# Norm boundaries of a two-layer encoder: half of the transposing products and zero-opened accumulators in the gap, the root from sums reduced early, weight conversions held behind, upper parts first

## The chip, the cores and the metric

One core of one Trainium2 chip. The metric is the device time of one execution in microseconds (us); lower is better. The core has TensorE (PE: matrix products; its weight loads are listed as PEld), VectorE (DVE), ScalarE (ACT), GpSimd (POOL) and SyncE (SP), whose queue issues most DMAs. Products accumulate in PSUM, which this kernel uses as eight buffers of 128 x 512 fp32 numbers; everything else on the core lives in SBUF.

## The reference

256 tokens of width 2048 pass through two layers. Layer 0 mixes tokens with a convolution module, layer 1 with gated linear attention (GLA); each layer then has a feed-forward with a short convolution. Every sub-layer f is wrapped in two norms and an adaptive modulation:

```python
h = _rms_norm(x, norm_g[i, 0]) * (1.0 + scale_m) + shift_m
y = mixer(h)                                    # conv module, or GLA
x = x + gate_m * _rms_norm(y, norm_g[i, 1])
h = _rms_norm(x, norm_g[i, 2]) * (1.0 + scale_f) + shift_f
y = _conv_ffn(h, ffn_w_in[i], ffn_conv_w[i], ffn_conv_b[i], ffn_w_out[i])
x = x + gate_f * _rms_norm(y, norm_g[i, 3])
```

`_rms_norm(x, g)` divides each token by the root of the mean of its squares plus 1e-6 and multiplies by g. Everything is fp32; the matrix products have to keep nearly that precision.

## The kernel before

**Products.** A weight block of 128 x 2048 is loaded whole (1 MB) by SP and split into an upper part `hi` (ACT casts it to the matmul format fp32r) and a lower part `lo` (DVE: weight minus upper part), in halves of 1024 columns (`Stream._process`, L120 and L122). Activations are split in the same way. A product takes three terms: hi x hi, hi x lo, lo x hi. `Stream` loads and converts the blocks in the order in which they will be used; `prepare(n)` converts the next n. Four `hi` and four `lo` buffers exist, so a conversion also waits until TensorE has done with a buffer.

**Two forms of product.** `mm_blocks` / `mm_block` (L410 to L427) has weights stationary and all 256 tokens moving: `act[k]` is 128 features x 512, the upper parts of 256 tokens (columns :T) and then the lower ones (T:), k running over 16 feature blocks. L421 multiplies `hi` with all 512 columns, L423 `lo` with the 256 upper ones. `mm_tokens` (L537) has tokens stationary: two tiles t = 0, 1 of 128 tokens; in the last column group of a projection (`last`) it finishes t = 0 first, then t = 1, and calls `each(t, ...)` behind each.

**A norm boundary** lies between a projection's last products and the next sub-layer's first. There are three: convolution module to feed-forward 0 (`proj_out`, near 463 us in the profile), feed-forward 0 to GLA (`ffn`, near 1213 us), GLA to feed-forward 1 (`proj_out`, near 1619 us). At each:

- `each` squares the projected row on ACT with a sum per column group (`token_squares`, L441; four sums per token in `ss`), and multiplies it by the gate (L594, or L905 and L912 in the feed-forward).
- `post_norm` (L564): `token_rstd` reduces the four sums (DVE, L448), takes the root (ACT, L449) and the reciprocal (DVE, L450); four instructions update x (L574); four squares of x follow; `token_diag` makes the second root in the same way and writes `dg[t]`, a diagonal matrix of 1/root (L480). `keep_clock` (L562) issues products whose result nobody reads: three on y and three on x at a boundary.
- `pre_norm` (L503) gives a list `Later`, filled on demand by `h_tiles` (L483): for two k at a time, four transposing products of x with `dg[0]` and `dg[1]` (L490), a modulation of 128 x 256 on ACT (`hn`, L497), and its split on DVE (cast L498, subtraction L499).
- The next sub-layer opens with two blocks side by side (`ps_fa` and `ps_fb`, or `ps_g` and `ps_q`), two k at a time, each pair of k behind `act.need`, which makes tiles some k ahead.

The order of each engine's instructions is set by a scheduler at build time: it takes the earlier line of the program first among what it believes to be ready. `tc.high_priority(n)` moves instructions n places ahead, `tc.issue_after(i)` keeps an instruction behind i on its engine. `st.hold` gives such bounds for the second block's conversions at a boundary:

```python
st.prepare(1, 0)
st.hold = (None, apool["x"]), (apool["sq"], apool["dg"])
st.prepare(2, 0)
```

The first pair is for the first half of the block (ACT free, DVE behind the last update of x), the second pair for the second half. PSUM has six buffers `ps` and one each of `ada` and `acc`.

## Time and profile before

| | us |
|---|---|
| median of 3 runs | 2377.85 (2375.11 to 2378.28) |
| profiled execution | 2375.24 |
| its span, first to last instruction | 2373.5 |
| TensorE busy | 2318.5 (98%) |
| DVE busy | 1767.1 (74%) |
| ACT busy | 1197.8 (50%) |
| mean granted TensorE clock | 0.99 |

A row of the timeline gives start, duration, engine, line of the kernel, operation, output<-inputs, shapes and count; merged rows have a count above 1, and their duration runs from the first start to the last end. What stands in square brackets is the engine's idle time before the row and what ended it. In a group's row stand total busy time, mean ns of one, and idle time before it by releaser. In the chain of waits, a row is start, duration and what the end of the program hung on then. A stretch's row gives its length, then per engine busy time and count, then granted clock, DMA share and GB/s. ACT's square with a sum is two rows: the instruction and a read of its accumulator.

### The profile page before, as it was taken

How to read it: one execution, taken by the hardware profiler on the slowest of the kernel's cores; microseconds unless marked ns; L12 is line 12 of the kernel's file. 1: busy time of each engine (PE TensorE's matmuls, PEld its weight loads, DVE VectorE, ACT ScalarE, POOL GpSimd, SP SyncE). 2: the span in 40 equal slices, each digit the busy share in tenths (PEclk: the TensorE clock that was granted, in tenths of full speed). 3: DMA queues.
4: the chain of work that ended last, by engine and by line, in shares of the span. 5: the costliest groups of instructions: out<-in, count | busy, mean ns of one | idle time of the engine just before them, and what ended most of it. 6: DMA issues, size and time to landing. Idle time of an engine off the chain costs nothing.

```text
span 2373.5 us, 34327 instructions
## 1 busy us (share of the span) xinstructions
PE 2318.5 (98%) x13616; PEld 1957.3 (82%) x13616; DVE 1767.1 (74%) x2531; ACT 1197.8 (50%) x1836; POOL 18.8 (1%) x43
## 2 busy tenths in 40 slices
PE   7999998899999999999999999999999999999998
PEld 5888756688878888888878888888888888888886
DVE  3879989678878888888877876756887466645665
ACT  5334354455534554345465576655554455544543
POOL 0000000000000000000000000000000000000000
PEclk8999999899999999999999999999999999999999
DMA  9978767657799878987947756463778555555553
GB/s 383 367 310 335 278 217 296 270 216 275 291 306 370 299 277 321 363 285 285 353 176 254 276 219 223 171 228 119 286 278 275 195 188 193 190 185 194 194 199 121
DMA packets 86721, 609.05 MB, mean 257 GB/s; under 512 B 10080, under 2 KB 10400, under 8 KB 13600
## 3 DMA queue, kind: packets, MB, share of 16 engines
q1 hardware_dynamic: 84944, 602.47, 69.0%
q0 software_dynamic: 1472, 4.23, 0.7%
q8 instruction: 106, 1.74, 0.3%
q14 instruction: 55, 0.45, 0.1%
q10 hardware_dynamic: 144, 0.16, 0.0%
HBM read 604.69 MB, written 2.13 MB: 256 GB/s over the span
## 4 chain that ended last, share of the span: by engine, by line
PE 90%; DVE 5%; DMA 3%; ACT 1%; issue 1%; SPq 0%; DVEq 0%; ACTq 0%
PE ps_fa L421 14%; PE ps_fb L421 14%; PE ps_fa L423 7%; PE ps_fb L423 7%; PE ps_fo L534 6%; PE ps_fo L535 6%; PE ps_fo L533 6%; PE ps_cin L793 3%; PE ps_cin L795 3%; PE ps_r L421 2%; PE ps_cin L794 2%; DMA raw<-in_adar 2%; PE ada L372 1%; PE ps_r L423 1%; DVE pair L724 1%; PE ps_q L421 1%
## 5 line engine op out<-in xcount | busy, mean ns | idle before, releaser
L122 DVE TENSOR_TENSOR lo<-raw,hi 128x1024 fp32r<-128x1024 f32 (+1 forms) x760 | 914.3, 1214 | 391.7 <-ACT hi L120 390.1
L120 ACT CAST hi<-raw 128x1024 fp32r<-128x1024 f32 (+1 forms) x760 | 784.0, 1042 | 809.0 <-PE ps_fa L421 191.3
L421 PE MATMUL ps_fa<-h,hi 128*128 128x512 f32 x1408 | 356.4, 393 | 0.4 <-ACT hn L497 0.4
L421 PE MATMUL ps_fb<-h,hi 128*128 128x512 f32 x1408 | 354.9, 392 | 0.0
L357 DVE CUSTOM_DVE_ANT_0 raw<-raw,cb 128x2048 f32<-128x2048 f32 x140 | 319.8, 2285 | 35.7 <-DMA raw<-in_adar 35.5
L421 PEld LDWEIGHTS ps_fa<-h,hi 128*128 128x128 f32 x1408 | 252.8, 189 | 45.7 <-DVE h L499 0.6
L421 PEld LDWEIGHTS ps_fb<-h,hi 128*128 128x128 f32 x1408 | 252.5, 189 | 44.2
L534 PE MATMUL ps_fo<-lo,u 128*128 128x512 f32 x704 | 274.4, 390 | 3.5 <-DVE lo L122 3.5
L535 PE MATMUL ps_fo<-hi,u 128*128 128x512 f32 x704 | 273.9, 389 | 0.0
L533 PE MATMUL ps_fo<-hi,u 128*128 128x512 f32 x704 | 273.2, 389 | 0.0
L423 PEld LDWEIGHTS ps_fa<-h,lo 128*128 128x128 f32 x1408 | 193.7, 190 | 15.1 <-DVE lo L122 0.5
L423 PEld LDWEIGHTS ps_fb<-h,lo 128*128 128x128 f32 x1408 | 193.7, 190 | 14.7
L423 PE MATMUL ps_fa<-h,lo 128*128 128x256 f32 x1408 | 198.3, 282 | 0.1
L423 PE MATMUL ps_fb<-h,lo 128*128 128x256 f32 x1408 | 198.2, 282 | 0.0
L534 PEld LDWEIGHTS ps_fo<-lo,u 128*128 128x128 f32 x704 | 132.2, 188 | 31.9 <-DVE lo L122 4.8
L535 PEld LDWEIGHTS ps_fo<-hi,u 128*128 128x128 f32 x704 | 132.1, 188 | 27.5
L533 PEld LDWEIGHTS ps_fo<-hi,u 128*128 128x128 f32 x704 | 132.2, 188 | 27.2
L793 PE MATMUL ps_cin<-h,hi 128*128 128x256 f32 x512 | 149.0, 294 | 5.7 <-ACT hi L120 3.3
L794 PE MATMUL ps_cin<-h,hi 128*128 128x256 f32 x512 | 146.4, 288 | 0.0
L795 PE MATMUL ps_cin<-h,lo 128*128 128x256 f32 x512 | 144.7, 288 | 1.2 <-DVE lo L122 1.2
L793 PEld LDWEIGHTS ps_cin<-h,hi 128*128 128x128 f32 x512 | 100.2, 196 | 22.1 <-ACT hi L120 10.7
L794 PEld LDWEIGHTS ps_cin<-h,hi 128*128 128x128 f32 x512 | 100.4, 196 | 0.9 <-DVE pair L704 0.8
(250 smaller groups left out, 2691.4 us busy)
## 6 DMA issues: line engine op xcount, KB each, us to landing
raw<-in_fin SPq DMA_DIRECT2D x176, 1024.0 KB, 4.9
raw<-in_adar SPq DMA_DIRECT2D x140, 1024.0 KB, 6.4
raw<-in_fout SPq DMA_DIRECT2D x88, 1024.0 KB, 5.5
raw<-in_adac SPq DMA_DIRECT2D x44, 1024.0 KB, 5.5
raw<-in_gin SPq DMA_DIRECT2D x33, 1024.0 KB, 5.5
raw<-in_cin SPq DMA_DIRECT2D x32, 1024.0 KB, 11.3
raw<-in_cout SPq DMA_DIRECT2D x16, 1024.0 KB, 8.0
raw<-in_gv SPq DMA_DIRECT2D x16, 1024.0 KB, 4.8
```

Of the source, the lines that this page charges most:

```text
L120: nc.scalar.copy(hi[:, :w], r[:, s : s + w])
L122: nc.vector.tensor_sub(lo[:, :w], r[:, s : s + w], hi[:, :w].bitcast(F32))
L357: V.tensor_tensor_reduce(out=r, in0=r, in1=cb, scale=1.0, scalar=0.0, op0=ALU.mult, op1=ALU.add, accum_out=mod[l, m][:, k : k + 1])
L372: nc.tensor.matmul(ps[32 * (j % 4) : 32 * (j % 4) + 32], cz[:, kt], r[:, j * n : (j + 1) * n], start=kt < 4, stop=kt >= KT - 4, tile_posit ...
L421: nc.tensor.matmul(ps, hi(k * P), act[k], start=k == 0, stop=False)
L423: nc.tensor.matmul(ps[:, :T], lo(k * P), act[k][:, :T], start=False, stop=k == nk - 1)
L533: nc.tensor.matmul(pv, ah, wh, start=kt == 0, stop=False)
L534: nc.tensor.matmul(pv, ah, wl, start=False, stop=False)
L535: apool["tok"] = nc.tensor.matmul(pv, al, wh, start=False, stop=kt == nk - 1)
L793: nc.tensor.matmul(ps[:, b], hi(o), ah, start=k == 0, stop=False)
L794: nc.tensor.matmul(ps[:, b], hi(o), al, start=False, stop=False)
L795: nc.tensor.matmul(ps[:, b], lo(o), ah, start=False, stop=k == nk - 1)
```

## The change

- **Root.** A new `most` adds the first three of the four sums on DVE and scales them; the root on ACT takes the fourth sum as input and the result of `most` as bias. For y it is made at column group 2, for x in `token_diag`.
- **Transposing products.** `pre_norm` now makes them itself: the ones of the first 128 tokens (t = 0), which need only `dg[0]`, for k = 0 to 11 at once, three PSUM banks of four k; those of k = 12 to 15 later. The ones of t = 1 come four k at a time (`make`), for k = 0 in a bank of its own.
- **Modulation.** One ACT instruction per k and t (128 x 128) instead of one per k, into tiles of the `y` pool; k = 0, t = 0 free, k = 1 and 2, t = 0 behind the root of t = 1, and so on in a written order.
- **Opening.** The two accumulators are opened by products of zeros, before the diagonal of t = 1; the first two k are multiplied upper half first (`hi` and `lo` with the upper activations), then `hi` with the lower ones. Later pairs of k as before, with `act.need(k0 + 4)`.
- **Held conversions.** The second block's first upper half goes behind the x root of t = 0, its lower half in two parts behind the last update of x and behind `dg[1]`; the second half goes behind the modulation and the subtractions of the first four k.
- **Clock products.** Those on y are gone; those on x use PSUM buffer `acc` instead of `ada`.

The diff, without the places where arguments are only passed on:

```diff
@@ -115,11 +115,13 @@
             with self.tc.high_priority(self.first):
-                a, v = self.hold[0 if s == 0 else 1] if self.hold else (None, None)
+                a, *vs = self.hold[0 if s == 0 else 1] if self.hold else (None, None)
                 with self.tc.issue_after(a.ins) if a else ExitStack():
                     nc.scalar.copy(hi[:, :w], r[:, s : s + w])
-                with self.tc.issue_after(v.ins) if v else ExitStack():
-                    nc.vector.tensor_sub(lo[:, :w], r[:, s : s + w], hi[:, :w].bitcast(F32))
+                n = w // len(vs)
+                for o, v in zip(range(0, w, n), vs):
+                    with self.tc.issue_after(v.ins) if v else ExitStack():
+                        nc.vector.tensor_sub(lo[:, o : o + n], r[:, s + o : s + o + n], hi[:, o : o + n].bitcast(F32))
             his.append(hi)
...
@@ -208,6 +210,8 @@
     G.memset(ones, 1.0)
+    zeros = const.tile([P, 1], F32R, tag="zeros", name="zeros")
+    G.memset(zeros.bitcast(F32), 0.0)
     epsb = const.tile([P, 1], F32, tag="epsb", name="epsb")
...
@@ -411,11 +415,24 @@
         parts = [st.get(key, 1 if key is keys[-1] else 0) for key in keys]
-        pss = [pp["ps"].tile([P, 2 * T], F32, tag="ps", name="ps_" + "_".join(map(str, key))) for key in keys]
-        run = 2 if isinstance(act, Later) and len(act) < nk else RUN
+        fresh = isinstance(act, Later) and len(act) < nk
+        pss = act.pss if fresh else [
+            pp["ps"].tile([P, 2 * T], F32, tag="ps", name="ps_" + "_".join(map(str, key))) for key in keys
+        ]
+        run = 2 if fresh else RUN
         for k0 in range(0, nk, run):
-            if isinstance(act, Later):
-                act.need(k0 + run + 2)
+            if fresh and k0:
+                act.need(k0 + 4)
+            elif fresh:
+                for k in range(run):
+                    for ps, (hi, lo) in zip(pss, parts):
+                        nc.tensor.matmul(ps[:, :T], hi(k * P), act[k][:, :T], start=False, stop=False)
+                        nc.tensor.matmul(ps[:, :T], lo(k * P), act[k][:, :T], start=False, stop=False)
+                for k in range(run):
+                    for ps, (hi, lo) in zip(pss, parts):
+                        nc.tensor.matmul(ps[:, T:], hi(k * P), act[k][:, T:], start=False, stop=False)
+                continue
             for ps, (hi, lo) in zip(pss, parts):
...
@@ -443,10 +460,16 @@
-    def token_rstd(ss, name):
+    def most(ss, name):
+        b = small.tile([P, 1], F32, tag="tb", name="tb" + name)
+        V.tensor_reduce(b, ss[:, :3], mybir.AxisListType.X, ALU.add)
+        V.tensor_scalar(b, b, 1.0 / D, EPS, ALU.mult, ALU.add)
+        return b
+    def token_rstd(ss, b, name):
         r = small.tile([P, 1], F32, tag="tr", name="tr" + name)
-        V.tensor_reduce(r, ss, mybir.AxisListType.X, ALU.add)
-        A.activation(r, r, AF.Sqrt, bias=epsb, scale=1.0 / D)
+        apool["root"] = A.activation(r, ss[:, 3:], AF.Sqrt, bias=b, scale=1.0 / D)
         V.reciprocal(r, r)
...
@@ -501,14 +524,67 @@
     def pre_norm(l, which, sh, sc, dg):
         add_bias(l, sh)
         add_bias(l, sc)
         scale_gain(l, which, sc)
         st.prepare(1, 0)
-        st.hold = (None, apool["x"]), (apool["sq"], apool["dg"])
+        x, one, root = apool["x"], apool["dg"], apool["root"]
+        fs, early = {}, {}
+        def product(n, k, t):
+            nc.tensor.matmul(n, X[t][k // 4][:, (k % 4) * P : (k % 4 + 1) * P], dg[t], start=True, stop=True)
+        def first(g):
+            pool, tag = (psum1, "ada") if g == 2 else (pp["ps"], "ps")
+            early[g] = pool.tile([P, 4, P], F32, tag=tag, name=f"ps_h{l}{which}_0_{g}")
+            for i in range(4):
+                product(early[g][:, i], 4 * g + i, 0)
+        def modulated(k, t, n):
+            if k // 2 not in fs:
+                fs[k // 2] = ypool.tile([P, 2, T], F32, tag="y", name=f"hn{l}{which}_{k}")
+            with tc.issue_after((apool["f"] if k > 2 else root).ins) if k and t == 0 else ExitStack():
+                apool["f"] = A.activation(fs[k // 2][:, k % 2, t * P : (t + 1) * P], n, AF.Identity,
+                                          bias=mod[l, sh][:, k : k + 1], scale=mod[l, sc][:, k : k + 1])
+        pss = [pp["ps"].tile([P, 2 * T], F32, tag="ps", name=f"ps_{l}{which}{i}") for i in range(2)]
+        for ps in pss:
+            nc.tensor.matmul(ps, zeros.to_broadcast([P, P]), zeros.to_broadcast([P, 2 * T]), start=True, stop=False)
+        for g in range(3):
+            first(g)
+        def make(k0):
+            if k0 == 8:
+                first(3)
+            rooms = [pp["ps"].tile([P, 4, P], F32, tag="ps", name=f"ps_h{l}{which}_1_{k0}{i}") for i in range(1 + (k0 == 0))]
+            ns = {k: rooms[-1 if k > k0 else 0][:, k - k0] for k in range(k0, k0 + 4)}
+            for k, n in ns.items():
+                product(n, k, 1)
+            order = ((0, 0), (1, 0), (2, 0), (0, 1), (1, 1), (3, 0), (2, 1), (3, 1))
+            for i, t in order if k0 == 0 else [(i, t) for t in range(2) for i in range(4)]:
+                k = k0 + i
+                modulated(k, t, ns[k] if t else early[k // 4][:, i])
+            hs = []
+            for k in ns:
+                f = fs[k // 2][:, k % 2]
+                hs.append(hpool.tile([P, 2 * T], F32R, tag="h", name=f"h{l}{which}_{k}"))
+                V.tensor_copy(hs[-1][:, :T], f)
+                apool["low"] = V.tensor_sub(hs[-1][:, T:], f, hs[-1][:, :T].bitcast(F32))
+            return hs
+        out = Later(make)
+        out.pss = pss
+        out.need(0)
+        st.hold = (apool["root0"], x, one), (apool["f"], apool["low"])
         st.prepare(2, 0)
         st.hold = None
-        return Later(lambda k: h_tiles(l, which, sh, sc, dg, range(k, k + 2)))
+        return out
...
@@ -555,21 +631,15 @@
-    def keep_clock(src, tag="ada"):
-        pool = psum1 if tag == "ada" else pp["ps"]
-        ps = pool.tile([P, 512], F32, tag=tag, name="clock")
+    def keep_clock(src):
+        ps = psum1.tile([P, 512], F32, tag="acc", name="clock")
         nc.tensor.matmul(ps[:, : src.shape[-1]], ident, src, start=True, stop=True)
-    def post_norm(l, which, t, ss, ys, last=False):
-        if t and not last:
-            for c in range(2):
-                keep_clock(ys[t, c])
-        r = token_rstd(ss[t], f"y{l}{which}{t}")
+    def post_norm(l, which, t, ss, b, ys, last=False):
+        r = token_rstd(ss[t], b, f"y{l}{which}{t}")
         sx = new_sums(f"x{l}{which}{t}")
-        if t and not last:
-            keep_clock(ys[t, 2])
         for c in range(4):
...
@@ -578,11 +648,16 @@
                     keep_clock(X[t][c])
-        return None if last else token_diag(sx[t], f"x{l}{which}{t}")
+        if last:
+            return None
+        d = token_diag(sx[t], f"x{l}{which}{t}")
+        if t == 0:
+            apool["root0"] = apool["root"]
+        return d
     def proj_out(name, act, l, which, gate, room=None):
         ss = new_sums(f"y{l}{which}")
-        ys, dg, gs = {}, {}, []
+        ys, dg, gs, bs = {}, {}, [], {}
         for c in range(4):
...
@@ -597,8 +672,10 @@
                     warm(AF.Sqrt, y)
+                if c == 2:
+                    bs[t] = most(ss[t], f"y{l}{which}{t}")
                 if c == 3:
-                    dg[t] = post_norm(l, which, t, ss, ys)
+                    dg[t] = post_norm(l, which, t, ss, bs[t], ys)
```

More of the change, by code (lines that the diff above doesn't have):

```diff
@@ L476, in token_diag @@
     def token_diag(ss, name):
-        r = token_rstd(ss, name)
+        r = token_rstd(ss, most(ss, name), name)
         dg = small.tile([P, P], F32, tag="dgx", name="dgx" + name, bufs=2)
@@ L909, in each @@
                                 warm(AF.Sqrt, ys[1, c])
+                            if c == 2:
+                                bs[t] = most(ss[t], f"y{l}3{t}")
                             y = pv if c == 3 else ys[t, c]
```

4 lines of the change are left out of this document (2 added, 2 removed).

## The prediction

> **What bounds the kernel now.** I read the page's engine shares and chain first, then the timeline around the first norm boundary engine by engine, then the chain of waits there, then the same places at the two other boundaries and the tail.
>
> ```profile
> PE 2318.5 (98%) x13616; PEld 1957.3 (82%) x13616; DVE 1767.1 (74%) x2531; ACT 1197.8 (50%) x1836; POOL 18.8 (1%) x43
> PE 90%; DVE 5%; DMA 3%; ACT 1%; issue 1%; SPq 0%; DVEq 0%; ACTq 0%
> ```
>
> TensorE carries the chain; what leaves it comes off the time unless another engine replaces it. At a boundary it loses time twice. First boundary, TensorE (a fp32 product is two records):
>
> ```profile
> 462.59 0.40 PE L535 MATMUL ps_cout<-hi,uc 128*128 128x512 f32 x1
> ...
> 466.27 3.49 PE L562 MATMUL clock<-x,ident 128*128 128x512 f32 x6
> ...
> 469.98 2.27 PE L490 MATMUL ps_h<-dgxx,x 128*128 128x128 f32 x18 [0.21 <-DVE dgxx L480]
> ...
> 472.45 0.47 PE L421 MATMUL ps_fa<-h,hi 128*128 128x512 f32 x1 [0.20 <-ACT hn L497]
> ...
> 488.38 1.99 PE L421 MATMUL ps_fa<-h,hi 128*128 128x512 f32 x8
> ```
>
> Useful work stops at 462.99 and resumes, with products that transpose x, at 469.98: the gap. From there to 488.38, where the second block of the feed-forward starts, is the opening: 18.40 us. The clock products in the gap do nothing for the result. ACT and DVE in the same place:
>
> ```profile
> 463.57 0.19 ACT L441 ACTIVATION_READ_ACCUMULATOR junk<-ps_cout 128x1 f32 x1
> 463.67 1.04 ACT L120 CAST hi<-raw 128x1024 fp32r<-128x1024 f32 x1
> 464.60 0.29 ACT L449 ACTIVATE try<-try,epsb 128x1 f32<-128x1 f32 x1
> ...
> 468.50 0.19 ACT L441 ACTIVATION_READ_ACCUMULATOR junk<-x 128x1 f32 x1
> 469.11 0.29 ACT L449 ACTIVATE trx<-trx,epsb 128x1 f32<-128x1 f32 x1 [0.42 <-DVE trx L448]
> 470.95 2.01 ACT L497 ACTIVATE hn<-ps_h,m,m 128x256 f32<-128x256 f32 x4 [1.55 <-PE ps_h L490]
> ...
> 480.10 1.99 ACT L120 CAST hi<-raw 128x1024 fp32r<-128x1024 f32 x2
> ```
>
> ```profile
> 463.80 0.69 DVE L594 TENSOR_TENSOR y<-ps_cout,gs 128x512 f32<-128x512 f32 x1 [3.09 <-ACT junk L441]
> ...
> 464.93 0.16 DVE L450 RECIPROCAL try<-try 128x1 f32<-128x1 f32 x1 [0.37 <-ACT try L449]
> 465.13 2.74 DVE L574 SCALAR_TENSOR_TENSOR x<-y,try,x 128x512 f32<-128x512 f32 x4
> 467.78 1.22 DVE L122 TENSOR_TENSOR lo<-raw,hi 128x1024 fp32r<-128x1024 f32 x1
> ...
> 469.63 0.29 DVE L480 TENSOR_SCALAR dgxx<-ident,trx 128x128 f32<-128x128 f32 x1
> ```
>
> The gap's chain: last square sum (463.76), a weight conversion that slipped in, root, reciprocal, four updates of x, four squares, sum (468.69), reduce on DVE, root, reciprocal, diagonal (469.92). The other boundaries, second then third:
>
> ```profile
> 1213.86 0.70 DVE L912 TENSOR_TENSOR ps_fo<-yf,g 128x512 f32<-128x512 f32 x1
> ...
> 1214.45 0.18 ACT L441 ACTIVATION_READ_ACCUMULATOR junk<-yf 128x1 f32 x1
> ...
> 1214.54 1.03 ACT L120 CAST hi<-raw 128x1024 fp32r<-128x1024 f32 x1
> ...
> 1215.48 0.29 ACT L449 ACTIVATE try<-try,epsb 128x1 f32<-128x1 f32 x1
> ...
> 1216.00 2.08 DVE L574 SCALAR_TENSOR_TENSOR x<-yf,try,x 128x512 f32<-128x512 f32 x3
> ...
> 1219.37 0.19 ACT L441 ACTIVATION_READ_ACCUMULATOR junk<-x 128x1 f32 x1
> ...
> 1220.50 0.29 DVE L480 TENSOR_SCALAR dgxx<-ident,trx 128x128 f32<-128x128 f32 x1
> ```
>
> ```profile
> 1618.33 0.40 PE L535 MATMUL ps_gout<-hi,o 128*128 128x512 f32 x1
> ...
> 1620.87 2.74 DVE L574 SCALAR_TENSOR_TENSOR x<-y,try,x 128x512 f32<-128x512 f32 x4
> ```
>
> From the last product to the first update the third takes 2.54 us, the first 465.13 - 462.59 = 2.54 too: I cost them alike.
>
> **The change, part by part.**
>
> *Root of y.* The first three sums are reduced early (two small DVE instructions per root, while TensorE still multiplies; DVE idled 3.09 us before L594), so the root needs only ACT's own last sum; the conversion at 463.67 (1214.54 in the second) is held back. Root at 463.80 instead of 464.60. But DVE does L594 until 464.49, so the reciprocal comes at about 464.45 and the updates at 464.65: 0.5 us gained. Second boundary: sum at 1214.63, root done 1214.96, DVE free from 1214.56, updates at 1215.2 instead of 1216.00: 0.8. If ACT must wait longer for its own sum than the 0.04 assumed, up to 0.2 of it goes.
>
> *Root of x.* Sum at 468.69, root at 468.73 instead of 469.11: 0.38; the second has the same 0.94 from 1219.56 to 1220.50. The lower-part conversion at 467.78 is halved, so the early reduction fits before the last sum. Together: 0.5 + 0.8 + 0.5 + 3 x 0.38 = 2.9 us.
>
> *Tail.* The last norm has no boundary behind it but the same root:
>
> ```profile
> 2365.46 0.19 ACT L441 ACTIVATION_READ_ACCUMULATOR junk<-yf 128x1 f32 x1
> ...
> 2365.87 0.29 ACT L449 ACTIVATE try<-try,epsb 128x1 f32<-128x1 f32 x1 [0.23 <-DVE try L448]
> ```
>
> 0.18 us of the 0.22 goes: 0.2.
>
> *Opening.* Prices of its work from the chain of waits:
>
> ```profile
> 477.26 0.47 PE ps_fa L421 x2
> 477.72 0.23 PE ps_fa L423 x2
> ...
> 478.65 0.89 PE ps_h L490 x8
> ```
>
> Before: 16 pairs of products at 0.70 = 11.2, and of 64 transposing records 58 after the diagonal (6 were done in the gap) at 0.111 = 6.45: 17.65, so 0.75 is idle, 0.47 of it before 472.45 (469.98 + 18 x 0.111 = 471.98). After: the half for the first 128 tokens needs only the earlier diagonal; 24 of its 32 records (2.7 us) and two zero products (0.23 each) go into the gap, 3.1 us. Three of six clock products a boundary are gone; the three on x stay, at 3.49. The gap left is about 6.1 (469.04 - 462.99), so 6.6 don't quite fit one after the other: if all early products run ahead of the clock products, these end 0.55 after the new diagonal; if they run in the pauses between them (a clock product keeps TensorE busy 2 x 4 x 0.111 = 0.89 of its 1.16), nothing is lost. I take 0.2 a boundary, 0.6 in all, nearer to the second, since the first clock product can start on its updated x near 465.4, before the early products are through. Left after the diagonal: 40 records, 4.45, so 15.65 of work, 2.0 less. Splitting the first two k into halves costs nothing: three 256-wide products instead of one 512 and one 256, at 0.23 for two.
>
> What hides the start: one product gives its result in about 0.45 (six took 469.98 to 470.95, five records less at 0.111), then 128 columns on ACT and one DVE cast: first product near diagonal + 1.35 instead of + 2.5, with 0.9 of remaining transposing products before it. That leaves idle like the old 0.47.
>
> What it costs elsewhere: ACT now modulates 32 halves instead of 16 blocks.
>
> ```profile
> L120 ACT CAST hi<-raw 128x1024 fp32r<-128x1024 f32 x742 | 772.1, 1049 | 805.6 <-PE ps_fa L421 191.3 <-PE ps_fo L535 150.0 <-PE ps_fb L421 127.9
> L120 ACT CAST hi<-raw 128x512 fp32r<-128x512 f32 x16 | 9.3, 616 | 3.4 <-DMA raw<-in_gout 2.1 <-DMA raw<-in_fout 1.2
> ...
> L498 DVE CAST h<-hn 128x256 fp32r<-128x256 f32 x64 | 17.7, 290 | 9.9 <-ACT hn L497 9.9
> ```
>
> A column costs (1049 - 616)/512 = 0.85 ns; four 256-wide modulations start 0.48 apart ((2.01 - 0.56)/3, the 0.56 being one by itself), so a half costs 0.48 - 0.11 = 0.37. ACT after the diagonal: 0.5 wait, five halves 2.2, held conversion 0.95, 24 halves 8.9, two conversions of the next block (480.10) 1.9: 14.5; then cast and subtraction, then the last pair's 1.0 to 1.4: end near 16.4, against 15.65 + 0.75 = 16.4 for TensorE. So both run level, ACT has no slack, and a conversion that comes in front of a block whose four early halves precede its first late half stalls TensorE by up to 1.3. Gain of an opening: between 0.7 (17.7) and 2.75 (no idle at all); I take 1.6, near the 2.0 less a third of that stall. Three: 4.8 us.
>
> The Trainium skill, "Perfetto Trace Analysis", section "Optimizing Scalar/DVE Operations", puts ScalarE's overhead per instruction on PSUM at about 51 ns. By it 16 more instructions cost 0.8 us an opening and ACT would not bind, an opening gains 2.0 and the whole sums to 8.5. The rows here have 0.27 fixed in 0.48, five times as much, and I go by them.
>
> *The held conversions.* The second block's upper half waits for four modulated blocks, its lower half for their subtraction: about diagonal + 5 instead of 469.83 + 1.22. They are needed for its ninth k, past + 9. Behind them SP's next load slips as much; it is for a block four ahead, tens of us away: nothing.
>
> **Sum.** 2.9 + 0.2 + 4.8 - 0.6 = 7.3 us against the profiled execution, 2375.24 (span 2373.5). The median shown is 2377.85, 2.6 above; I take the same 7.3 from it: 2370.6 (rounded up from 2370.55). A change under 0.2% (4.8 us) can't be told from none: the three runs span 3.2.
>
> **The rivals.**
> *ACT or DVE binds the opening.* For it: ACT's 14.5 of 16.4 above, and DVE, which adds 0.29 + 0.42 a block and three conversions. Against: it idled before most modulations before. Openings then gain 0 to 0.5: 2.5 to 4.0 us in all, 2373.9 to 2375.4, no telling difference.
> *The early products don't go in the gap* (TensorE's order puts them behind the clock products on x, which wait for updates until about 467): 2.7 us of products end past the new diagonal at 469, by 1.2; openings gain 2.0 - 1.2 = 0.8 each instead of 1.6 - 0.2, 1.8 less in all: 2372.4. It lies in the likeliest range.
> *Slower: the clock drops.* TensorE has fewer fillers.
>
> ```profile
> 412.74 1.94 PE L372 MATMUL ada<-raw,cz 128*32 128x512 f32 x8 [5.28 <-DMA raw<-in_adac]
> 415.00:425.00 10.00, 6.09 (x17) 4.41 (x18) 8.45 (x7) 1.99 (x2) 0.00 (x0) 0.58 1.01 420
> ```
>
> After 5.28 us of idleness the granted clock was 0.58 over 10 us: 4.2 us lost. At three boundaries 12.6 - 7.3 = 5.3 slower, 2383.2. It decides once TensorE idles that long; I work out at most 2.4 (from 463.0 to the first clock product on an updated x near 465.4) and only if the early products come late.
> The Trainium skill, "TensorE: Matmul & The Clock Gate", Part 1, lets one idle window of about 3.4 us halve the clock: that would bring the point closer, still past 2.4. By that rule this rival keeps its small chance.
>
> **How the numbers follow.** Likeliest 0.66, the early products' order among it (own range 2366.5 to 2373.0: openings of 2.75 with no clock loss, 11.4 in all; openings of 0.7 with half the sum's loss, 4.9); ACT or DVE binds 0.21; the clock, or an order of instructions that goes wrong as dearly, 0.08; nothing gained, because the boundaries' time comes back in the blocks behind, 0.05. The range 2366.5 to 2376.5 takes in the second and leaves out the last two, 0.13. Faster by over 0.2% (below 2373.1): 0.66. Slower: 0.08. The rest, 0.26.
>
> **What would show it.** Right: root of y within 0.1 us of the last sum at each boundary; diagonal 0.9 to 1.2 earlier after the last product; 24 transposing records between the zero products and the diagonal; first product 1.2 to 1.9 after the diagonal; from the diagonal to the second block about 16.8; granted clock 1.00. Wrong: ACT back to back through the opening with TensorE waiting for modulated blocks, early products behind the diagonal, or a clock under 1.00 at a boundary.

## The result, and the profile after

| | median, us | range | profiled execution | span |
|---|---|---|---|---|
| before, same chip | 2377.18 (4 runs) | | 2375.24 | 2373.5 |
| changed | 2358.46 (4 runs) | 2353.49 to 2360.2 | 2360.2 | 2358.5 |

The ratio is 0.9918, 95% interval 0.9902 to 0.9934: 18.7 us faster, where 7.3 were forecast and 2366.5 was the lower end of the range. A second measurement of the same kernel gave 2356.01, ratio 0.991 (0.9896 to 0.9923). So the prediction was wrong. The boundaries gained about what was predicted; the larger part of the gain came from elsewhere.

The changed kernel's page, engine shares and the chain by engine:

```profile
PE 2301.0 (98%) x13616; PEld 1935.1 (82%) x13616; DVE 1767.7 (75%) x2550; ACT 1208.9 (51%) x1884; POOL 16.8 (1%) x44
...
PE 91%; DVE 4%; DMA 3%; issue 1%; ACT 1%; SPq 0%; another core or an unknown queue 0%; DVEq 0%; ACTq 0%
```

TensorE still carries the chain. Its busy time fell by 17.5 us. The nine clock products that are gone kept it busy for 9.8 us of that; the rest is a first sign that products which the change doesn't touch have come closer together.

Changed kernel, timeline of TensorE at the first boundary (start, us, engine, line, operation, count):

```profile
459.76 0.40 PE L611 MATMUL ps_cout<-hi,uc 128*128 128x512 f32 x1
460.00 0.60 PE L556 MATMUL ps<-zeros 128*128 128x512 f32 x2
460.43 2.17 PE L537 MATMUL ps_h<-dgxx,x 128*128 128x128 f32 x18
462.52 1.12 PE L637 MATMUL clock<-x,ident 128*128 128x512 f32 x2
...
464.88 1.12 PE L637 MATMUL clock<-x,ident 128*128 128x512 f32 x2
465.85 1.95 PE L537 MATMUL ps_h<-dgxx,x 128*128 128x128 f32 x12
467.63 0.39 PE L430 MATMUL ps<-h,hi 128*128 128x256 f32 x1
...
478.67 0.86 PE L438 MATMUL ps_fa<-h,hi 128*128 128x512 f32 x3
...
480.86 0.39 PE L438 MATMUL ps_fa<-h,hi 128*128 128x512 f32 x1
...
483.41 1.09 PE L438 MATMUL ps_fa<-h,hi 128*128 128x512 f32 x4
```

The zero products and 24 transposing records (18, 2, 2 and the first two of the last 12) stand in the gap, before the new diagonal ends at 466.21; the first product that uses a modulated block starts at 467.63. At 478.67 and 480.86 TensorE already runs products of the second block inside the opening (`ps_fa`; the opening's own accumulators are named `ps`).

Changed kernel, timeline of ScalarE: first boundary, then the second, then the tail:

```profile
460.69 0.19 ACT L458 ACTIVATION_READ_ACCUMULATOR junk<-ps_cout 128x1 f32 x1
460.92 0.29 ACT L472 ACTIVATE try<-ssy,tby 128x1 f32<-128x1 f32 x1
...
465.08 0.19 ACT L458 ACTIVATION_READ_ACCUMULATOR junk<-x 128x1 f32 x1
465.40 0.29 ACT L472 ACTIVATE trx<-ssx,tbx 128x1 f32<-128x1 f32 x1
...
469.79 5.37 ACT L550 ACTIVATE hn<-ps_h,m,m 128x128 f32<-128x128 f32 x15
475.19 2.00 ACT L120 CAST hi<-raw 128x1024 fp32r<-128x1024 f32 x2
...
1208.25 0.19 ACT L458 ACTIVATION_READ_ACCUMULATOR junk<-yf 128x1 f32 x1
1208.47 0.29 ACT L472 ACTIVATE try<-ssy,tby 128x1 f32<-128x1 f32 x1
...
2350.71 0.19 ACT L458 ACTIVATION_READ_ACCUMULATOR junk<-yf 128x1 f32 x1
2350.93 0.29 ACT L472 ACTIVATE try<-ssy,tby 128x1 f32<-128x1 f32 x1
```

Each root of y now starts 0.03 to 0.04 us after the end of its last sum (460.88, 1208.44, 2350.90).

Changed kernel, VectorE at the first boundary:

```profile
461.71 2.74 DVE L644 SCALAR_TENSOR_TENSOR x<-y,try,x 128x512 f32<-128x512 f32 x4
464.37 0.69 DVE L124 TENSOR_TENSOR lo<-raw,hi 128x512 fp32r<-128x512 f32 x1
...
465.15 0.15 DVE L467 TENSOR_SCALAR tbx<-tbx 128x1 f32<-128x1 f32 x1
...
465.92 0.29 DVE L503 TENSOR_SCALAR dgxx<-ident,trx 128x128 f32<-128x128 f32 x1
```

From the last product (459.76) to the first update of x are 1.95 us, before 2.54; to the end of the diagonal 6.45, before 7.33 (469.92 - 462.59).

And now the surprise. Here is the chain of waits in the middle of a feed-forward, far from any boundary; each piece is eight products, 512 columns wide (first line of a pair, "wide" from here on) or 256 (second, "narrow"). The kernel before:

```profile
522.04 1.84 PE ps_fa L421 x8
523.88 0.95 PE ps_fa L423 x8
```

The changed kernel, the same two kinds of piece:

```profile
521.46 1.86 PE ps_fb L438 x8
523.32 0.91 PE ps_fb L440 x8
```

Eight narrow products take 0.04 less, eight wide ones 0.02 more. From the starts of all such records (starts 300 ns or more apart are left out): a 256-wide product behind another starts 118.9 ns after it in the kernel before and 114.1 in the changed one (mean of 2440 and 2408); 512 behind 512 took 230.6 and now 232.3, the change from 512 to 256 took 227.2 and now 235.8. No line of the change touches these products. The convolution module's input projection (`ps_cin`), whose products are all 256 wide, ends at 257.1 instead of 263.0 us, before the first boundary has begun. These distances between starts are called paces below.

### The profile page after: what moved, and what is told of

It is laid out like the page before. It is cut to its first block, busy times and chain, and to the rows that moved or that the text cites. A ratio compares the mean times of both kernels' runs of the same rounds, so it can differ in the third digit from the quotient of the medians.

```text
span 2358.5 us, 34325 instructions
## 1 busy us (share of the span) xinstructions
PE 2301.0 (98%) x13616; PEld 1935.1 (82%) x13616; DVE 1767.7 (75%) x2550; ACT 1208.9 (51%) x1884; POOL 16.8 (1%) x44
## 4 chain that ended last, share of the span: by engine, by line
PE 91%; DVE 4%; DMA 3%; issue 1%; ACT 1%; SPq 0%; another core or an unknown queue 0%; DVEq 0%; ACTq 0%
PE ps_fb L438 14%; PE ps_fa L438 13%; PE ps_fa L440 7%; PE ps_fb L440 7%; PE ps_fo L610 7%; PE ps_fo L611 7%; PE ps_fo L609 7%; PE ps_r L438 3%; PE ps_cin L870 2%; PE ps_cin L872 2%; PE ps_cin L871 2%; DMA raw<-in_adar 2%; PE ada L376 1%; DVE pair L801 1%; PE ps_k L438 1%; PE ps_r L440 1%
## 5 line engine op out<-in xcount | busy, mean ns | idle before, releaser
L438 PE MATMUL ps_fa<-h,hi 128*128 128x512 f32 x1376 | 348.7, 395 | 0.0
L438 PE MATMUL ps_fb<-h,hi 128*128 128x512 f32 x1376 | 348.1, 395 | 0.0
L438 PEld LDWEIGHTS ps_fa<-h,hi 128*128 128x128 f32 x1376 | 246.1, 188 | 46.1
L438 PEld LDWEIGHTS ps_fb<-h,hi 128*128 128x128 f32 x1376 | 245.8, 188 | 45.8
L440 PEld LDWEIGHTS ps_fa<-h,lo 128*128 128x128 f32 x1376 | 182.5, 188 | 16.0 <-DVE lo L124 0.5
L440 PEld LDWEIGHTS ps_fb<-h,lo 128*128 128x128 f32 x1376 | 182.5, 188 | 15.6
L440 PE MATMUL ps_fa<-h,lo 128*128 128x256 f32 x1376 | 185.0, 277 | 0.0
L440 PE MATMUL ps_fb<-h,lo 128*128 128x256 f32 x1376 | 184.8, 277 | 0.0
L870 PEld LDWEIGHTS ps_cin<-h,hi 128*128 128x128 f32 x512 | 98.6, 193 | 22.3 <-ACT hi L120 10.9
L872 PEld LDWEIGHTS ps_cin<-h,lo 128*128 128x128 f32 x512 | 98.0, 194 | 2.0 <-DVE lo L124 2.0
```

The lines of the kernel that those rows point to most:

```text
L438: nc.tensor.matmul(ps, hi(k * P), act[k], start=k == 0, stop=False)
L440: nc.tensor.matmul(ps[:, :T], lo(k * P), act[k][:, :T], start=False, stop=k == nk - 1)
L870: nc.tensor.matmul(ps[:, b], hi(o), ah, start=k == 0, stop=False)
L872: nc.tensor.matmul(ps[:, b], lo(o), ah, start=False, stop=k == nk - 1)
```

## The experiments

What the change does to these products was found in the built programs: its two new small tiles, `zeros` in the constants and `tb` among the small tiles, take 32 and 64 bytes of every partition, and all pools behind them move up. (Addresses are read from the allocation of the built program; no trace shows them.) The activations `h` start at byte 48160 before and 48192 after, the halves of the weights, `hi` and `lo`, at 138528 before and 138624 after. Theory A: these addresses set the pace, and the boundaries gained what was forecast. Theory B: the addresses do nothing, and the pace came with the new order of instructions or from the chip. Every comparison is of five rounds; ratios are to the kernel before on the same chip.

**The kernel before, with unused bytes that put every pool where the change puts it** (each unused tile is also set to zero once; those lines are left out here and below).

```diff
+    padc = const.tile([P, 8], F32, tag="padc", name="padc")
+    pads = small.tile([P, 16], F32, tag="pads", name="pads", bufs=1)
```

> The kernel before, with 32 unused bytes per partition in the constants and 64 in the small pool, so that every later buffer starts where the changed kernel has it (activations at 64 beyond a multiple of 128 bytes, weight halves at 0; before: both at 32). Nothing else differs. Theory A (the part of the gain that I did not forecast comes from these addresses: TensorE's 256-wide products start 113 ns apart instead of 120): 256-wide pace 114 ns on average, time 8 to 11 us below the kernel before, near 2367. Theory B (the pace comes with the new order of instructions, or from chip to chip): pace 119, time as before within 2 us.

Measured: 2364.49 us, ratio 0.9955 (0.9943 to 0.9968), 10.8 us less than the 2375.27 of the kernel before beside it, by 96 unused bytes. Its chain in the same place:

```profile
521.80 1.86 PE ps_fa L425 x8
523.66 0.91 PE ps_fa L427 x8
```

The paces are the changed kernel's (114.2, 232.2, 235.7), the gaps those of the kernel before (diagonal 7.32, 8.08 and 7.32 us after the last product). This is what theory A expected.

**The change at exactly the old addresses:** both new tiles live in an existing slot.

```diff
-    table = const.tile([P, 1], F32, tag="table", name="table")
+    table = small.tile([P, 1], F32, tag="warm", name="warm")
-        b = small.tile([P, 1], F32, tag="tb", name="tb" + name)
+        b = small.tile([P, 1], F32, tag="warm", name="tb" + name)
```

> The changed kernel with every pool at exactly the byte at which the kernel before has it (the two small tiles that the change adds share a slot that exists). The first try at this kept the remainders by 128 but moved the weight halves by 128 bytes, and its pace was neither kernel's. Theory A, now with the addresses alone (pace by the places of activations and weights together): 256-wide 119, 512-wide 231 and 227, as before; time 7 to 9 us below the kernel before, 2366 to 2368, which is what was forecast for the change without addresses. Rival: the order of the instructions needs the new addresses, and this run is no faster than the kernel before, like the first try (2379).

Measured: 2369.74 us, ratio 0.9967 (0.9954 to 0.9979), 8.1 us less than the 2377.8 beside it. Paces as before (119.0, 230.5, 226.7). This is the change as the prediction saw it, and 2370.6 was forecast. The change alone and the addresses alone multiply to 0.9967 x 0.9955 = 0.9922, and the two measurements of the changed kernel, which has both, gave 0.9918 and 0.991.

**Which address matters?** First one operand was moved at a time in the kernel before, then both were put at their old remainders by 128 in the changed one:

```diff
 # activations to 48192, weights to 138656
+    padc: 32 bytes in const;  pads: 96 bytes in small
 # activations stay at 48160, weights to 138560
+    pads: 32 bytes in small
 # changed kernel, activations at 48160, weights at 138656
-    table in const
+    table in the slot "warm";  pads: 64 bytes in small
```

> The kernel before with the activations h moved by 32 bytes to a multiple of 64, and the weight halves left at 32 beyond one. In a 256-wide product h is the moving operand and the weights are loaded. If the moving operand's address sets the pace: all of the first run's gain, 256-wide pace 114. If the loaded one's: none, pace 119.

> The kernel before with the weight halves (and the feed-forward's activations u) moved to a multiple of 64 bytes and the activations h left. If the moving operand's address sets the pace of the 256-wide products: no gain there, pace 119; in the token form (weights moving, 512 wide, 227 ns in both kernels) no change either. If the loaded operand's: all of the first run's gain.

> The changed kernel with every buffer at the address that it had before (one constant moved to the small pool, 64 unused bytes there). Theory A: 256-wide pace 119, and of the 18.7 us gained 8 to 11 are lost: near 2368, which leaves 7 to 10 for what I forecast at 7.3. Theory B: 2358, pace 114.

All three went elsewhere than expected: 2388.13 (ratio 1.0049, 1.0037 to 1.0062), 2385.79 (1.0044, 1.0032 to 1.0057) and 2378.86 (1.0013, 1.0004 to 1.0022). The narrow products ran 118.3, 119.4 and 118.6 ns apart, near the 118.9 of the kernel before, and the wide ones 233.8, 232.9 and 232.9, further apart than in both kernels. Chain of the first of them:

```profile
521.44 1.87 PE ps_fb L425 x8
523.31 0.94 PE ps_fb L427 x8
```

So neither operand's own address decides, nor both remainders by 128. What differs in all five layouts is the distance from the activations to the weights: 90368 before, 90432 in the changed kernel, 90464, 90400 and 90496 in these three. The next two test it.

**The same distance elsewhere, and the old distance elsewhere.**

```diff
 # everything 32 bytes up (distance 90432 as in the changed kernel)
+    padc: 32 bytes in const
 # activations alone 64 bytes up (distance 90368 as before)
+    padc: 64 bytes in const;  tb in the slot "warm"
```

> The changed kernel with 32 more bytes in front of everything: activations at 48224, halves of the weights at 138656, so their distance is as in the changed kernel (90432) and their remainders by 128 are 96 and 32. Theory D (the distance sets the pace): 256-wide products still 114 ns apart and the changed kernel's time, within 2 us. Theory R (the place of each operand by itself, by its remainder, sets it): another pace, and a time 5 to 25 us longer, as in the runs with the weights at 138656 before (118.3 to 118.6 ns, 2379 to 2388 us).

> The changed kernel with the activations alone moved up by 64 bytes, to 48256, a multiple of 128, and the halves of the weights where they are (138624, also a multiple of 128). Theory R (the remainders count, and a multiple of 128 is the best place): 256-wide products at 114 ns or less, and 512-wide at 230 or less: as fast as the changed kernel or up to 10 us faster. Theory D (the distance counts): it is 90368, that of the kernel before, so 119 ns and about 230.6, and 2368 to 2372 us. Rival: any move of one operand alone is slower, as in the two runs that moved one (about 10 us).

Measured: 2355.74 (0.992, 0.9907 to 0.9934) and 2367.09 (0.9967, 0.9955 to 0.9979). Paces 114.1, 232.3, 235.8 in the first, 119.0, 230.6, 226.7 in the second: to a tenth those of the changed kernel at the same two distances. The chain of the second, whose addresses are both multiples of 128:

```profile
520.98 1.84 PE ps_fa L440 x8
522.82 0.95 PE ps_fa L442 x8
```

Among these layouts the distance alone goes with the pace. Theory R of the expectation, by which a multiple of 128 is a good place for each operand by itself, falls.

**How it depends on the distance:** unused bytes between the two, in the changed kernel.

```diff
+    pads = small.tile([P, n // 4], F32, ...)   # n = 128, 192, 256; 512 at the old addresses; 96, 160
```

> The changed kernel with 128 unused bytes between activations and weights: distance 90560, remainder 192 by 256 and 448 by 512, which no run has had. By symmetry about the remainder 256 of the kernel before (448 is as far from it as 64), no theory has a pace for it; between 114 and 120 ns for 256-wide products, so 2356 to 2380 us. What it tells: whether a remainder other than the changed kernel's reaches 114 ns.

> The changed kernel with 192 unused bytes: distance 90624, remainder 0 by 256 and by 512. Theory P256 (the pace comes back every 256 bytes): that of the kernel before, 119 ns, 230.6 and 227, and 2366 to 2370 us. Theory P512 (every 512 bytes): another pace. The output products of the feed-forward, whose operands lie 32768 apart (also 0 by 512), ran 226.9 ns apart for 512 columns in every run, so there 512-wide products near 227.

> The changed kernel with 256 unused bytes: distance 90688, remainder 64 by 256 and by 512. Theory P256: the changed kernel's pace, 114 ns, 232.3 and 236, and 2355 to 2360 us. Theory P512: another pace, and a time more than 3 us away.

> The changed kernel at the addresses of the kernel before, with 512 unused bytes between activations and weights: distance 90880, as in the kernel before 256 by 512 and 0 by 256. Theories P256 and P512 both: the paces of the kernel before (119 ns, 230.6, 227) and 2367 to 2371 us. If the whole distance counts, and not its remainder, another pace.

> The changed kernel with 96 unused bytes: distance 90528, remainder 160 by 256. If the pace moves smoothly between its neighbours 128 (118.6 ns for 256 columns behind 256, 232.9 for 512 behind 512, 230.9 at the change from 512 to 256; 2378.9 us) and 192 (115.8, 228.7, 230.3; 2354.4 us): near 117, 231 and 230.6, and some 2365 us. If only multiples of 64 are good places: as 32 and 96 (118.3 to 119.4, 232.9 to 233.8) and 2372 to 2382 us.

> The changed kernel with 160 unused bytes: distance 90592, remainder 224 by 256. If the pace moves smoothly between its neighbours 192 (115.8, 228.7, 230.3; 2354.4 us) and 0 (119.0, 230.5, 226.7; 2366 to 2370 us): near 117.4, 229.6 and 228.5, and some 2360 us. If only multiples of 64 are good places: 118.3 to 119.4, 232.9 to 233.8 and 2372 to 2382 us. A better place than any before would be under 2352 us.

Mean start to start (ns) of the feed-forward's input products (`ps_fa`, `ps_fb`), by the remainder of the distance by 256; times of the changed kernel, but for 32 and 96, where the kernel before was run:

| remainder | distances run | 256 behind 256 | 512 behind 512 | 512 to 256 | us |
|---|---|---|---|---|---|
| 0 | 90368, 90624, 90880 | 119.0 | 230.6 | 226.7 | 2369.74, 2367.09; 2366.79; 2365.81 |
| 32 | 90400 | 119.4 | 232.9 | 231.8 | (2385.79) |
| 64 | 90432, 90688 | 114.1 | 232.3 | 235.8 | 2358.46, 2356.01, 2355.74; 2354.23 |
| 96 | 90464 | 118.3 | 233.8 | 233.6 | (2388.13) |
| 128 | 90496 | 118.6 | 232.9 | 230.9 | 2378.86 |
| 160 | 90528 | 119.7 | 233.4 | 231.4 | 2384.51 |
| 192 | 90560 | 115.8 | 228.7 | 230.3 | 2354.37 |
| 224 | 90592 | 117.2 | 233.3 | 234.1 | 2373.16 |

The period of 256 held at the two remainders where it was tried: 90624 and 90880 run like 90368, and 90688 like 90432 (with 2365.81 and 2354.23 us, 90880 and 90688 came out about 1 us below their expected ranges). The other remainders were run at one distance each. Between neighbours the pace isn't smooth: 160 and 224 came out near 2384.5 and 2373.2 us, not 2365 and 2360, and their wide products (233.4 and 233.3) are as slow as at 32 and 96. The other theory of these two runs, that multiples of 64 alone are good places, missed its own ranges too: 160 came out above them (119.7 ns, 2384.51 us), and the narrow pace of 224 below (117.2 ns). By it 128 should be fast, and it isn't (2378.86 us). So no simple rule was found. The chain at remainder 192, which no kernel had by itself:

```profile
522.78 1.83 PE ps_fb L440 x8
524.61 0.91 PE ps_fb L442 x8
```

The kernel at 192 came out a little below its expected 2356 to 2380. The fastest medians, 2354.23 (0.9911, 0.9898 to 0.9924) and 2354.37 (0.9909, 0.9896 to 0.9922), can't be told from the changed kernel's. From the best remainder to the worst, 64 to 160, lie some 26 to 30 us of the same instructions.

**The boundary's parts,** all at the changed kernel's addresses, to be held against its 2356.01 to 2358.46. The stretch from the last product of the output projection to the first feed-forward output product, which holds a whole boundary and 32 blocks, is compared too, since it doesn't vary by more than 0.03 us between runs with the same instructions and the same distance: 193.4 before, 192.2 with the new addresses alone, 190.35 with the change at the old ones, 189.1 with both.

*The old opening and the old holds,* with the early root kept (`pre_norm` and the order of the products as before the change, each `lo` in one piece held as before, clock products of y still gone).

> The changed kernel with the openings and held conversions of before (transposing products two k at a time, modulations 256 wide, no zero products, accumulators opened by the first real product); the early root, the missing clock products on y and the new addresses stay. By my sum the openings were worth 1.6 - 0.2 each; the traces of after and of the first run (same addresses) put a boundary's whole gain at 3.0, of which 0.9 to 1.2 is before the diagonal, so about 2 each: 4 to 6 us slower than the changed kernel. If the clock needs the products on y, more: 2 to 4 each boundary, with a granted clock under 1 behind it.

Measured: 2365.78 (0.9955, 0.994 to 0.997), no better than the unused bytes alone, and 9.8 us above the changed kernel beside it, where 4 to 6 were expected; the stretch takes 192.9. The three boundaries are 3.8, 3.0 and 3.3 longer than in the changed kernel, 10.1 in all. Some 2 of each are the opening, as expected. The diagonals, which the expectation left out, make another 1.1 each: they end 7.51, 8.26 and 7.50 us after the last product, even 0.2 later than before the change. The early root gained nothing here: the conversion is again ahead of it, and a whole `lo` ahead of the early reduction.

```profile
455.64 0.19 ACT L445 ACTIVATION_READ_ACCUMULATOR junk<-ps_cout 128x1 f32 x1
455.73 1.03 ACT L120 CAST hi<-raw 128x1024 fp32r<-128x1024 f32 x1
456.66 0.30 ACT L459 ACTIVATE try<-ssy,tby 128x1 f32<-128x1 f32 x1
```

The last half us is the clock, at the first boundary alone. TensorE, then a window there (start:end, length, busy time of the five engines, granted clock, DMA share, GB/s):

```profile
458.00 5.08 PE L573 MATMUL clock<-x,ident 128*128 128x512 f32 x6 [2.23 <-DVE x L580]
```

```profile
459.40:462.80 3.40, 3.34 (x4) 0.93 (x4) 2.91 (x7) 1.64 (x5) 0.00 (x0) 0.50 0.00 0
```

Behind 2.23 us without a product the granted clock was 0.50 from 459.4 to 462.8; at the third boundary, behind 2.22, it stayed 1.00. In the changed kernel the early transposing products fill this part of the gap in place of the clock products of y, and the clock stays 1.00 at every boundary.

*The old root,* everything else kept:

```diff
-        apool["root"] = A.activation(r, ss[:, 3:], AF.Sqrt, bias=b, scale=1.0 / D)
+        V.tensor_reduce(r, ss, mybir.AxisListType.X, ALU.add)
+        apool["root"] = A.activation(r, r, AF.Sqrt, bias=epsb, scale=1.0 / D)
```

> The changed kernel with the root made from all four sums as before (reduction on DVE between last sum and root); the openings stay, and so do the early additions, unused. My terms: 0.2 to 0.4 at each of six roots on the path, and 0.2 at the tail: 1.5 to 2.5 us slower than the changed kernel. If the held conversion was what delayed the root, half of that.

Measured: 2359.57 (0.9922, 0.9909 to 0.9935), 1 to 4 us slower by the medians, with overlapping intervals; the trace is clearer. The diagonals end 7.22, 7.27 and 7.22 us after the last product, against 6.45, 7.12 and 6.45: the early root is worth 0.77, 0.15 and 0.77. The holds without it are worth 0.11, 0.82 and 0.11.

*No holds:*

```diff
-        st.hold = (apool["root0"], x, one), (apool["f"], apool["low"])
+        st.hold = None
```

> The conversions of the next two weight blocks are held behind nothing; the rest of the change and its addresses stay. Theory (the holds keep ScalarE and VectorE free for the roots and diagonals, as the earlier diagonals of the changed kernel suggest): a conversion of some 1 us slips ahead of a root, or of the diagonal, at each of the three boundaries; the diagonal comes 0.5 to 1.2 us later and the kernel is 1.5 to 4 us slower than the changed one (about 2359). Rival (the scheduler would place them behind the roots by itself, and the opening, not the hold, is what matters): within 1 us of the changed kernel, with the diagonal within 0.1 us of its place.

Measured: 2360.28 (0.9936, 0.9924 to 0.9949), 2 to 4 us slower by the medians; the diagonals end at 7.81, 8.61 and 7.81, 1.4 late at each boundary, more than the 0.5 to 1.2 expected, since both engines are late. ScalarE, then VectorE:

```profile
457.77 0.19 ACT L458 ACTIVATION_READ_ACCUMULATOR junk<-ps_cout 128x1 f32 x1
457.86 1.04 ACT L120 CAST hi<-raw 128x1024 fp32r<-128x1024 f32 x1
458.79 0.29 ACT L472 ACTIVATE try<-ssy,tby 128x1 f32<-128x1 f32 x1
```

```profile
458.93 1.23 DVE L124 TENSOR_TENSOR lo<-raw,hi 128x1024 fp32r<-128x1024 f32 x1
460.07 0.15 DVE L473 RECIPROCAL try<-try 128x1 f32<-128x1 f32 x1
```

*No clock products:*

```diff
-                if t and c < 3:
-                    keep_clock(X[t][c])
```

> The three clock products on the running sums of each boundary are left out, so that nothing but the two zero products and the twelve early transposing products of the lower tokens is in the gap. Theory (work inside the gap keeps the granted clock, the lower tokens' products are enough only from the moment their diagonal is there): TensorE is idle for some 4 to 5 us in the gap; if the granted clock falls for it, the products behind the gap run at half pace for some 3 us and the kernel is 3 to 6 us slower than the changed one. Rival (the clock stands such a gap): the same time as the changed kernel within 0.6 us, with granted clock 1.00 behind each gap.

Measured: 2356.17 (0.992, 0.9908 to 0.9933), the same time by this measurement. But the trace doesn't bear out the rival, that the clock stands the gap. TensorE at the first two boundaries, then windows around them:

```profile
453.81 2.84 PE L537 MATMUL ps_h<-dgxx,x 128*128 128x128 f32 x24
459.64 1.77 PE L537 MATMUL ps_h<-dgxx,x 128*128 128x128 f32 x10 [3.00 <-DVE dgxx L503]
...
1203.16 2.94 PE L537 MATMUL ps_h<-dgxx,x 128*128 128x128 f32 x24 [1.27 <-DVE dgxx L503]
1208.25 2.49 PE L537 MATMUL ps_h<-dgxx,x 128*128 128x128 f32 x10 [2.14 <-DVE dgxx L503]
```

```profile
459.00:463.00 4.00, 3.36 (x19) 3.29 (x20) 3.27 (x10) 3.38 (x9) 0.00 (x0) 0.72 0.00 0
...
461.00:463.00 2.00, 2.00 (x11) 2.00 (x11) 1.92 (x6) 2.00 (x5) 0.00 (x0) 0.50 0.00 0
...
1208.00:1212.00 4.00, 3.75 (x18) 3.75 (x19) 2.60 (x8) 2.47 (x8) 0.00 (x0) 0.57 0.00 0
```

After 3.00 us without a product the granted clock is 0.72 over four us (0.57 after the second gap), and the stretches across the three boundaries are 1.4, 0.9 and 1.2 us longer: 3.5, inside what the clock theory expected. It doesn't show in the medians, whose intervals could hide it. In the two profiled executions it is mostly made up for before the boundaries: in the run with everything 32 bytes up, of the same paces, the granted clock is 0.50 from 160.8 to 164.2 us, inside the input projection, which here keeps 1.00 there. The Trainium skill, "TensorE: Matmul & The Clock Gate", Part 1, says that one idle window of about 3.4 us halves the clock and that the window doesn't start with the kernel; the 0.50 from 461 to 463 agrees in size, while here 3.00 and 2.14 us without a product were enough, the second behind 1.27 us of idleness and 2.94 us of transposing. So the three clock products on x save some 3.5 us of boundary time by the trace; that the kernel as a whole is faster with them is not shown.

## Why the prediction was wrong

**The step that failed** is the costing of the change's parts: the two small tiles, `zeros` and `tb`, were not costed at all. What fills them is small, but their 96 bytes moved every operand of TensorE behind them, and that was worth 10.8 us by itself, more than the whole sum. None of the rivals had it. No row of the profile before could have priced it; the sum should have had a term with no known sign for everything that moves when a tile is added, and the range should have reached further down, and up too: the change puts 64 bytes between activations and weights, and 32 or 96 there cost the kernel before 10.5 and 12.9 us by the medians (0.44% and 0.49%).

Where the 10.8 lie, by the trace of the kernel before with the unused bytes: the input projection ends 4.9 us earlier (258.15 against 263.02); the six stretches of feed-forward blocks (32, 32 and 24 blocks in each layer) are 0.9 to 1.2 shorter, 6.7 in all; the first layer's last output stage is 1.2 shorter. Against it stand 2.1 us between the input projection and the last product of the output projection and 0.5 from the second boundary to the third, in part because the other 512-wide products (`ps_cout`, `ps_v`) start 1.5 to 1.8 ns later each, and 3.8 in the first feed-forward output stage, which takes 93.8 us instead of 90.0. Summed, 4.9 + 6.7 + 1.2 - 2.1 - 0.5 - 3.8 = 6.4, and the two profiled spans differ by 6.8. The window of that output stage in this run and in the kernel before, then a part of it in this run:

```profile
652.00:745.90 93.90, 89.99 (x387) 73.94 (x386) 70.10 (x66) 36.27 (x41) 1.18 (x1) 0.96 0.94 337
```

```profile
656.00:746.00 90.00, 87.47 (x387) 71.89 (x386) 69.32 (x66) 35.25 (x41) 1.18 (x1) 1.00 0.96 339
```

```profile
676.60:683.40 6.80, 5.35 (x13) 4.19 (x14) 6.80 (x8) 2.96 (x4) 0.00 (x0) 0.50 0.96 360
```

The 3.8 is a longer wait and the clock: TensorE waits 3.9 us here for the lower part of a weight block (2.5 in the kernel before), and the granted clock is 0.50 for 6.8 us. The addresses alone don't decide this loss. The run at distance 90688, with the changed kernel's pace, passes the stage in 89.8 us at full clock, and the change at the old addresses takes 91.7 at 0.98. Without this loss the spans would differ by 6.8 + 3.8 = 10.6, near the 10.8 of the medians; the profiled run was the slowest of its five (2368.45).

**The rest, without the addresses, stood.** 8.1 us (interval 5.0 to 10.9) against 7.3; the three other kernels with the change at remainder 0 gave 0.996 to 0.9967, the same.

- *Roots:* the gaps are 0.88, 0.97 and 0.88 shorter, 2.73 against 2.9 (2.63 at the old addresses). The small miss is in x: its root starts 0.13 us after the last sum (465.27), behind the early reduction (465.30), which the halved conversion kept waiting until 464.97. The credit was shared differently than told: at the second boundary nearly all of it is the held conversion, which gains 0.82 there without the early root, at the others the early root. The early root gained nothing with the holds of before, or with none.
- *Tail:* 0.23 us between the sum's end and the root before, 0.03 now: the 0.2 forecast.
- *Early products:* 24, 20 and 24 of them in the gap, run before the first clock product and between the others; the last clock product ends at 466.00, before the diagonal at 466.21. The 0.6 taken off was not lost, except for the four records (4 x 0.111 = 0.44) that come too late at the second boundary.
- *Openings:* whole boundaries are 3.0, 2.7 and 3.0 us shorter at the old addresses, less 0.9 each for the gap: 2.1, 1.8 and 2.2, 6.1 in all, where 4.8 - 0.6 = 4.2 was forecast. That is the 2.0 each that the working had before it took off a third of a stall (0.4 each) and 0.2 for the early products. First products came 1.42, 1.79 and 1.42 after the diagonal. The term was too small because of the stall that was taken off it: ScalarE indeed is the bound in places (a window of the opening shows it busy 9.97 of 10 us, halves 0.35 us apart where 0.37 was worked out, and two conversions ahead of a block's halves at 475.19):

```profile
470.00:480.00 10.00, 10.00 (x65) 8.73 (x65) 9.01 (x23) 9.97 (x26) 0.00 (x0) 1.00 0.33 112
```

  but TensorE is busy throughout. While the next halves are missing it runs products of the second block, whose operands are ready, in the order that the scheduler gave it: `ps_fa` at 478.67, and again at 480.86. The second block goes on at 483.41, 17.2 after the diagonal's end (466.21); at the old addresses it is 17.2 too (488.62 - 471.39). Less four products of that block inside, at 0.23, that is 16.3, where 16.8 was forecast. The rival by which ScalarE binds had the mechanism right and its price wrong.
- *Clock:* 1.00 at every boundary; the rival needed a gap with less in it. Its price was too high: 0.9 to 1.4 us a boundary in the run without the clock products, not 4.2. The 4.2 counted all ten us of its window, of which TensorE worked only 6.09. And 2.23 us without a product sufficed once, less than the 2.4 that was thought safe.

## What to carry to other kernels

A tile added or resized, however small, moves everything that is allocated behind it, unless it shares a slot that exists; where TensorE is the bound, compare start-to-start times of products that the change doesn't touch before crediting the change, and run the old kernel with the new addresses (a few unused bytes) as a control. A root moved earlier pays only if other work is kept out of its way on both engines. Where an engine falls short for a moment inside a stage, ask what ready work the one that waits for it could run instead.

## What the hardware showed that was not expected

In the feed-forward's input products the time between two products goes with the distance in SBUF between the first bytes of the moving and the stationary operands, with a period of 256 bytes at the two remainders where that was tried, and not smoothly: 114.1 to 119.7 ns for 256 columns, 228.7 to 233.8 for 512 behind 512. Every tile of either kind starts a multiple of 2048 bytes from its pool's first, and each weight slice a multiple of 512 further, so one remainder holds for all these pairs. The output products of the feed-forward, whose operands lie 32768 bytes apart in every kernel, ran 226.8 to 227.0 ns apart in all of them. The Trainium skill, "TensorE: Matmul & The Clock Gate", "Back-to-back issue gap", gives N / 2.4 GHz + 2.5 ns for a single gap, by which an estimate for 256 and 512 columns is 109 and 216 ns, and says that the weight loads enter the spacing of a real stream; all runs here stay above those, and differ among themselves by more than the 2.5 ns. Why the distance matters was not settled: the traces show when products start, not what SBUF serves when.
